# Idle products at the start, copies of gated banks, later squares of finished rows, and another order of the last block in a transformer-layer kernel

## The chip, the core and the metric

The kernel runs on one core of a Trainium2 chip. The time is the device time of one execution in microseconds; lower is better. Before the change it is 2542.43 us, the median of 3 runs (2542.26 to 2542.9).

Five engines work at once, each through its own queue in order: TensorE (PE, products), VectorE (DVE), ScalarE (ACT), GpSimd (POOL) and SyncE (SP), which issues most DMAs. A PE product adds `weights.T @ moving` into a bank of PSUM of 128 x 512 numbers; its weight load is shown as PEld.

## What is computed

One layer of a streaming encoder on x (2048 tokens of width 1024), all in float32:

```python
u = rms_norm(h, g_mix_pre)
z = u @ w_in                                  # 2816 columns: q, k, v, qh, fh, ih, gh
ya = swa_with_sinks(q, k, v, sinks)           # 8 heads, sliding window of chunks of 64
yh = hgrn2(qh, fh, ih, gh, lb, onorm)         # 4 heads, gated linear recurrence, chunkwise
y = concatenate([ya, yh]) @ w_out
h = h + rms_norm(y, g_mix_post)
u = rms_norm(h, g_x_pre); m = rms_norm(mem, g_mem)
y = cross_attention(u, m, wq, wk, wv, wo)     # 4 heads, 256 memory tokens
h = h + rms_norm(y, g_x_post)
u = rms_norm(h, g_ffn_pre)
y = (silu(u @ w_gate) * (u @ w_up)) @ w_down  # inner width 2816
h = h + rms_norm(y, g_ffn_post)
```

## The kernel before

**Products in three parts.** PE's fast format is fp32r. Each operand is split into `hi` (a copy rounded to fp32r) and `lo` (the rest), and a product is three: hi x hi, hi x lo, lo x hi. Those are lines 1167, 1168 and 1169 (`products`); the stationary side is a streamed tile S, the moving side a tile T. `split2` (L1027) makes the halves: `hi` on ACT (L1030) or POOL (L1032), `lo` always on DVE (L1033).

**Blocks.** The large matrix products run in blocks of two by two quarters. `seven` (L1171) computes such a block from seven products of combined quarters in place of eight; `STEPS` (L1023) gives the order of the seven for each kind of block. One step is one quarter product, 4 x 3 = 12 PE products where the inner width is 4 tiles. Products 1, 6, 7 and 4 gather in one PSUM bank, 5 and 3 in a second, 2 in a third. `copy` (L1178) takes the partial sums of 1, 6 and 5 out of their banks (L1182 on ACT; L1184 on DVE where a part of the result is added), and `out` gets the four results: (0,0) after product 2, (1,1) after 7, (0,1) after 3, (1,0) after 4. Kinds "o", "s" and "d" are such blocks; "d" runs two blocks at once, step by step. Kinds "p" and "q" use `eight` (L1211), plain products without sums. `streamed` (L1109) loads the S side and yields its halves in the order of the steps.

**The order of the work.** `phases` (L1248) runs all blocks of a list of jobs, step by step. After each step's products it makes the S tiles of two steps ahead (`upto(g + 2)`), advances what follows earlier blocks by one `yield` each (`after`), and splits and fetches the T tiles of later steps (`split`, `half`), so that one `yield` in an `after` is one step of PE. The rows that `after` handles and the fetched halves of T share nine buffers (`row_tile`, L1492). The whole program is one Tile program whose planner, from a model of times, sets the final order on each engine; `behind` (L1093) holds instructions behind others of their engine.

**The stages**, in order:

1. `in_first` (L445) projects the first 1024 tokens, 11 pairs of columns, from x itself, transposed on the host. The first three pairs are blocks of kind "p" whose rows aren't normed yet. `first(q, s)` splits one quarter of x into `hi` and `lo` in four chunks, each scaled by the gain (L468 on ACT, L469 on DVE). The loads are queued on SP by hand: the gain, the first weight block (`load` in `in_block`, L576), the four chunks of the first quarter of x (`between`), the second weight block, and so on.
2. `in_proj` projects the second 1024 tokens while attention and recurrence of the first run. `in_cols` (L708) multiplies 128 columns (L720, L721, L723) into a PSUM bank of kind "g", of which there are two. ACT takes its tanh (L728); for columns of qh and gh DVE then multiplies `(tanh + 1) * bank` (L733), reading the bank once more. Columns of fh get POOL's affine map, and their decays use tiles of tag "u".
3. Then come attention and recurrence of the rest, and the folding of the cross-attention's weights (`fold_cross`).
4. Three jobs of eight blocks of two token tiles (256 tokens): the out projection (`mixed_block`, L1541), the scores (`score_block`) and the values (`value_block`, L1623).
5. The feed-forward: hidden blocks for each half of the tokens, and three jobs of down blocks (`down_block`, L1726).

**After a block of 4** (L1554 and L1638). `squared` (L1528) writes a finished quarter into its row tile (L1532, L1534) and takes its squares on ACT (L1510). POOL turns the sums into a reciprocal root, DVE scales the rows (L1557, L1641), POOL issues a DMA that adds the residual from memory to the row (L1539), and SP stores it. Then, for n below 12, `rest` follows after one more `yield`: ACT's squares of the new row (L1510 by `mean_squares`), the root, in the value blocks a second scaled row (L1662), PE's transposes (L1421), ACT's copies out (L1422) and the store of the transposed row to `h1t_d` or `u_d`. For n of 12 and 14 `rest` runs beside the next job.

```python
            if n < NT - 4:
                yield
                yield from rest()
```

**The end.** The last down block (n = 14) writes the output. Each finished quarter (L1754, L1756) is squared on ACT (L1510) and multiplied by the gain (L1763); once both quarters of a row are there, POOL makes the root (L1766, L1769), DVE scales and adds the residual in two halves (L1772), and SP stores each.

Of the kernel before, what the change touches and what calls it, by code (L numbers as in the profile page):

```python
# [14 lines left out]
AF = mybir.ActivationFunctionType  # L15
ALU = mybir.AluOpType
AX = mybir.AxisListType

P = 128
T = 2048  # L20
# [8 lines left out]
NPB = TB // P  # L29
# [4 lines left out]
C_KA, C_VA, C_QH, C_FH, C_IH, C_GH = 512, 640, 768, 1280, 1792, 2304  # L34
# [14 lines left out]
class Layer:  # L49
# [229 lines left out]
    def consts(self):  # L279
        nc = self.nc  # L280
        self.ident = self.cst.tile([P, P], F32, name="ident")
        make_identity(nc, self.ident)
        self.mhalf = self.cst.tile([P, 8], F32, name="mhalf")
        nc.vector.memset(self.mhalf, -0.5)


# [158 lines left out]
    def in_first(self):  # L445
# [4 lines left out]
        u = [[], []]  # L450
        T, raw, second, stage = {}, {}, {}, []
        key = {(0, 0): 1, (1, 0): 2, (0, 1): 8, (1, 1): 3}
        self.r_bc = self.r_half = None
        self.held = True

        def tile():
            return self.pair_tile().rearrange("p a d -> p (a d)").rearrange("p (k t) -> p k t", k=4)

        def x_load(q, s):
            for k in range(4):  # L460
                self.load(raw[q, s][:, k, :], I["x_t"][2 * s + q, :, k, :])
# [74 lines left out]
        def parted():  # L536
            for n in (1, 3, 2, 0):
# [5 lines left out]
                with self.behind() if n else contextlib.nullcontext():  # L543
# [6 lines left out]
        blocks = [("p" if i < 3 else "o",)  # L550
                  + self.in_block(*p, beside[i], get if i > 6 else (), None if i else lambda: x_load(0, 0))
                  for i, p in enumerate(self.ORDER)]
# [22 lines left out]

    def in_block(self, ca, cb, beside, get, between):  # L576

# [130 lines left out]
    def in_cols(self, b, u, cols, e1):  # L708
        nc = self.nc
        w = []  # L710
        for c in cols:
            w.append(self.wcols(self.I["w_in"], c))
        z = [self.io_tile("z") for _ in cols]
        for s in range(TB // 512):
            sl = slice(s * 512, (s + 1) * 512)
            for i, c in enumerate(cols):
# [10 lines left out]
                else:  # L727
# [4 lines left out]
                    else:  # L732
                        nc.vector.scalar_tensor_tensor(zs, zs, 1.0, ps, ALU.add, ALU.mult)  # L733
                        if c0 < C_FH:
# [287 lines left out]

    STEPS = {"o": (1, 5, 6, 3, 7, 2, 4), "s": (1, 2, 5, 6, 7, 3, 4), "d": (1, 2, 5, 6, 7, 3, 4), "p": (1, 2, 8, 3), "q": (1, 2, 8, 3)}  # L1023
    TAKES = {"o": (1,) * 7, "s": (1,) * 7, "d": (1,) * 7, "p": (2, 2, 0, 0), "q": (4, 0, 0, 0)}
    BLOCK = {1: (0, 0), 8: (0, 1), 2: (1, 0), 3: (1, 1)}
# [83 lines left out]
    def streamed(self, load, nk, kind, engine=None, tiled=False):  # L1109
# [100 lines left out]

    def eight(self, S, T, nk, out, addend, halves=False):  # L1211
        a11, a21 = S[:2]
        x, y = self.bank("g"), self.bank("t")
# [214 lines left out]
    def jobs(self):  # L1428
# [112 lines left out]
    def mixed_block(self, n):  # L1541
# [12 lines left out]
        def after():  # L1554
# [6 lines left out]
            if n < NT - 4:  # L1561
                yield
                yield from rest()
# [59 lines left out]
    def value_block(self, n):  # L1623
# [14 lines left out]
        def after():  # L1638
# [6 lines left out]
            if n < NT - 4:  # L1645
                yield
                yield from rest()
# [186 lines left out]
```

## Time and profile before

| | us |
|---|---|
| median of 3 runs | 2542.43 |
| profiled execution | 2546.34 |
| its span, first to last instruction | 2544.6 |
| PE busy in the span | 2504.1 |
| DVE busy | 1765.3 |
| ACT busy | 1247.3 |
| POOL busy | 459.0 |

The mean granted TensorE clock of that execution is 0.998.

All lines come from one profiled execution, with times in us from the start of its span. A row of the timeline reads: start, duration, engine, line, operation, output <- inputs, shapes, and how many instructions were put together; in brackets the idle time of the engine before it and what ended it. SPq is SyncE issuing a DMA. "S L1030" as a releaser is the instruction of line 1030 that writes S.

### The profile page before, as it was taken

The page shows a single profiled execution, that of the slowest core. Times are in us where ns is not written, and L with a number is a line of the kernel's source. Part 1 is how long each engine was busy: PE and PEld are TensorE (multiplying, and loading weights), DVE is VectorE, ACT ScalarE, POOL GpSimd, SP SyncE. Part 2 cuts the span into 40 slices and gives each one's busy share as a digit, 9 for nine tenths or more (in the row PEclk, how much of TensorE's full clock was granted, in tenths as well). Part 3 has the DMA queues.
Part 4 walks back from the last instruction along what each step waited for, and adds up shares of the span by engine and source line. Part 5 has one row for each costly group of instructions (what it writes and reads, how often), then busy time and mean ns, then how long its engine had stood idle before and what let it go on. Part 6 is the DMA issues. An engine that isn't in the chain of part 4 may idle for free. (4 is left out here: it accounts for less than half of the span.)

```text
span 2544.6 us, 34410 instructions
## 1 busy us (share of the span) xinstructions
PE 2504.1 (98%) x12164; PEld 2096.0 (82%) x12164; DVE 1765.3 (69%) x2813; ACT 1247.3 (49%) x2598; POOL 459.0 (18%) x641
## 2 busy tenths in 40 slices
PE   8999999999999999999999999999999999999998
PEld 6777889988988878888788888888888888888786
DVE  6869587788777587787775665586566566665756
ACT  5454465566655566655554333353333344533443
POOL 2233233222422243233210000000000000000022
PEclk9999999999999999999999999999999999999999
DMA  6263544567896795859964532254555433667798
GB/s 240 96 216 139 174 141 137 170 201 223 292 326 211 208 288 176 299 174 265 302 206 143 180 132 92 91 177 151 177 207 187 153 132 135 209 199 203 218 223 209
DMA packets 267852, 490.00 MB, mean 193 GB/s; under 512 B 20640, under 2 KB 125088, under 8 KB 267168
## 3 DMA queue, kind: packets, MB, share of 16 engines
q1 hardware_dynamic: 253856, 438.52, 51.0%
q0 software_dynamic: 12672, 46.14, 9.0%
q10 hardware_dynamic: 1152, 3.15, 0.3%
q8 instruction: 96, 1.57, 0.3%
q14 instruction: 76, 0.62, 0.1%
HBM read 326.26 MB, written 161.48 MB: 192 GB/s over the span
## 5 line engine op out<-in xcount | busy, mean ns | idle before, releaser
L1167 PE MATMUL psm<-T,S 128*128 128x512 f32 x2744 | 1063.5, 392 | 9.8 <-ACT S L1030 3.8
L1168 PE MATMUL psm<-T,S 128*128 128x512 f32 x2744 | 1070.8, 390 | 0.0
L1169 PE MATMUL psm<-T,S 128*128 128x512 f32 x2744 | 1064.0, 391 | 4.4 <-DVE S L1033 4.1
L1167 PEld LDWEIGHTS psm<-T,S 128*128 128x128 f32 x2744 | 516.1, 188 | 121.7 <-ACT S L1030 5.2
L1169 PEld LDWEIGHTS psm<-T,S 128*128 128x128 f32 x2744 | 515.8, 188 | 116.3 <-DVE S L1033 9.0
L1168 PEld LDWEIGHTS psm<-T,S 128*128 128x128 f32 x2744 | 516.1, 188 | 106.3
L1030 ACT ACTIVATE S<-sum 128x512 fp32r<-128x512 f32 (+1 forms) x336 | 206.2, 618 | 328.8 <-PE psm L1169 326.7
L1033 DVE TENSOR_TENSOR S<-sraw,S 128x512 fp32r<-128x512 f32 (+1 forms) x312 | 211.1, 684 | 214.7 <-ACT S L1030 193.6
L1033 DVE TENSOR_TENSOR S<-sum,S 128x512 fp32r<-128x512 f32 (+1 forms) x400 | 272.0, 685 | 77.9 <-ACT S L1030 62.8
L1182 ACT ACTIVATE part<-psm 128x512 f32<-128x512 f32 x294 | 173.5, 593 | 184.2 <-PE psm L1169 181.0
L1030 ACT ACTIVATE S<-sraw 128x512 fp32r<-128x512 f32 (+1 forms) x271 | 165.6, 616 | 163.0 <-PE psm L1169 148.4
L1539 POOL DMA_DIRECT2D row<-y_d x28 | 25.0, 893 | 1072.4 <-DMA sraw<-hid_d 905.3
L1510 ACT ACTIVATE junk<-row 128x512 f32<-128x512 f32 x160 | 99.7, 625 | 95.7 <-DVE row L1532 33.2
L1033 DVE TENSOR_TENSOR T<-row,T 128x1024 fp32r<-128x1024 f32 x104 | 125.2, 1211 | 30.6 <-ACT T L1030 30.3
L1030 ACT ACTIVATE T<-row 128x1024 fp32r<-128x1024 f32 x104 | 105.5, 1024 | 27.2 <-DMA row<-in_w_down_dram 11.0
L720 PE MATMUL psg<-u,whi 128*128 128x512 f32 x288 | 115.8, 402 | 1.7 <-ACT z L726 1.3
L721 PE MATMUL psg<-u,whi 128*128 128x512 f32 x288 | 115.5, 401 | 0.0
L153 DVE TENSOR_TENSOR wlo<-raw,whi 128x1024 fp32r<-128x1024 f32 x54 | 70.5, 1310 | 32.1 <-ACT whi L150 14.8
L1714 DVE TENSOR_TENSOR part<-psm,part 128x512 f32<-128x512 f32 x66 | 45.5, 689 | 65.5 <-PE psm L1169 65.4
L1705 DVE TENSOR_TENSOR row<-psm,part 128x512 f32<-128x512 f32 x66 | 45.5, 689 | 53.8 <-PE psm L1169 53.8
L723 PE MATMUL psg<-u,wlo 128*128 128x512 f32 x288 | 79.9, 403 | 0.7 <-DVE wlo L153 0.7
L1032 POOL TENSOR_SCALAR S<-sum 128x512 fp32r<-128x512 f32 x64 | 49.2, 774 | 170.6 <-PE psm L1169 147.3
(347 smaller groups left out, 3562.2 us busy)
## 6 DMA issues: line engine op xcount, KB each, us to landing
sraw<-in_w_gate_dram SPq DMA_DIRECT2D x44, 512.0 KB, 4.8
sraw<-in_w_up_dram SPq DMA_DIRECT2D x44, 512.0 KB, 5.0
hid_d<-row SPq DMA_DIRECT2D x44, 512.0 KB, 2.7
h_d<-row SPq DMA_DIRECT2D x32, 512.0 KB, 7.1
y_d<-row SPq DMA_DIRECT2D x32, 512.0 KB, 3.8
sraw<-hid_d SPq DMA_DIRECT2D x32, 512.0 KB, 5.4
row<-h_d POOLq DMA_DIRECT2D x30, 512.0 KB, 7.9
row<-y_d POOLq DMA_DIRECT2D x28, 512.0 KB, 7.1
```

The source lines that it names most:

```text
L153: nc.vector.tensor_tensor(lo, raw, f32(hi), ALU.subtract)
L720: nc.tensor.matmul(ps, w[i][0][:, k, :], u[s][k][0], start=(k == 0), stop=False)
L721: nc.tensor.matmul(ps, w[i][0][:, k, :], u[s][k][1], start=False, stop=False)
L723: nc.tensor.matmul(ps, w[i][1][:, k, :], u[s][k][0], start=False, stop=(k == KT - 1))
L1030: self.nc.scalar.activation(hi, raw, AF.Copy)
L1032: self.nc.gpsimd.tensor_scalar(hi, raw, 1.0, 1.0, ALU.mult, ALU.mult)
L1033: self.nc.vector.tensor_tensor(lo, raw, f32(hi), ALU.subtract)
L1167: nc.tensor.matmul(ps, s[:, 0, k, :], t[:, 0, k, :], start=st, stop=False, **kw)
L1168: nc.tensor.matmul(ps, s[:, 0, k, :], t[:, 1, k, :], start=False, stop=False, **kw)
L1169: nc.tensor.matmul(ps, s[:, 1, k, :], t[:, 0, k, :], start=False, stop=sp, **kw)
L1182: nc.scalar.activation(t, ps, AF.Copy)
L1510: self.nc.scalar.activation(junk, a, AF.Square, scale=float(D) ** -0.5, accum_out=to)
```

## The change

There are six edits.

- **Early activation.** `consts` has ACT copy four numbers of `mhalf`, which DVE has set, to a small tile.
- **Idle products.** `in_first` starts with eleven PE products of `ident` with itself (128 x 128, float32), all into one PSUM bank that nothing reads.
- **Load order and `eight`.** Of the four chunks of x, the first is loaded behind the first weight block and the other three behind the second. In `eight`, the first two products of a "p" block run interleaved: for each of the four inner tiles, the three products of `a11` and the three of `a21`, in place of all twelve of `a11` and then all of `a21`.
- **Gated banks.** In `in_cols`, for qh and gh, ACT also copies the bank into a tile of tag "u", and DVE's multiply reads that copy.
- **Later squares.** For n = 8 and 10 of the out projection and the values, `rest` follows after three yields in place of one.
- **Last block.** The last down block has the kind "e": product 3 stands before product 7, and so do its S tiles (`streamed`); `TAKES` gets the same entry as the kinds beside it.

```diff
         nc.vector.memset(self.mhalf, -0.5)
+        nc.scalar.activation(self.small("w_mn", 4), self.mhalf[:, 0:4], AF.Copy)
...
         self.held = True
+        idle = self.bank("h")
+        for _ in range(11):
+            nc.tensor.matmul(idle[:, 0:P], self.ident, self.ident, start=True, stop=True)
...
-        def x_load(q, s):
-            for k in range(4):
+        def x_load(q, s, ks=range(4)):
+            for k in ks:
...
-                  + self.in_block(*p, beside[i], get if i > 6 else (), None if i else lambda: x_load(0, 0))
+                  + self.in_block(*p, beside[i], get if i > 6 else (), () if i else ((0,), (1, 2, 3)), x_load)
...
             for i, c in enumerate((ca, cb)):
-                if between and i and not j:
-                    between()
                 self.load(t[:, i, :], w[c, :, j * 512:(j + 1) * 512])
+                if between and not j:
+                    x_load(0, 0, between[i])
...
+        gated = not (cols[0] * P < C_QH or C_FH <= cols[0] * P < C_GH)
+        pre = self.io_tile("u") if gated else None
...
-                        nc.vector.scalar_tensor_tensor(zs, zs, 1.0, ps, ALU.add, ALU.mult)
+                        nc.scalar.activation(pre[:, sl], ps, AF.Copy)
+                        nc.vector.scalar_tensor_tensor(zs, zs, 1.0, pre[:, sl], ALU.add, ALU.mult)
...
+    STEPS = {..., "e": (1, 2, 5, 6, 3, 7, 4), ...}
...
-            yield made(combine(a11, a21, ALU.subtract), "P")
-            yield made(combine(a12, s2, ALU.subtract), "A")
+            last = [(a11, a21, "P"), (a12, s2, "A")]
+            for a, b, e in reversed(last) if kind == "e" else last:
+                yield made(combine(a, b, ALU.subtract), e)
...
-            self.products(x, [(a11, T[1], nk)], True, False)
-            self.products(y, [(a21, T[1], nk)], True, False)
+            kw = dict(skip_group_check=True)
+            for k in range(nk):
+                for ps, s in ((x, a11), (y, a21)):
+                    nc.tensor.matmul(ps, s[:, 0, k, :], T[1][:, 0, k, :], start=not k, stop=False, **kw)
+                    nc.tensor.matmul(ps, s[:, 0, k, :], T[1][:, 1, k, :], start=False, stop=False, **kw)
+                    nc.tensor.matmul(ps, s[:, 1, k, :], T[1][:, 0, k, :], start=False, stop=False, **kw)
...
-            last = "dd" if c + 1 < len(down) else ""
+            last = "dd" if c + 1 < len(down) else "e"
...
             if n < NT - 4:
-                yield
+                for _ in range(3 if n >= NPB else 1):
+                    yield
                 yield from rest()
```

The last hunk stands in `mixed_block` and in `value_block`. Before, the last block of the last job had kind "s": products 1, 2, 5, 6, 7, 3, 4.

More of the change, by code (lines that the diff above doesn't have):

```diff
@@ L574, in in_first, with in_block @@
         return u
-    def in_block(self, ca, cb, beside, get, between):
+    def in_block(self, ca, cb, beside, get, between, x_load):
         nc, w = self.nc, self.I["w_in"]
@@ L1016, in swa @@
             yield
-    STEPS = {"o": (1, 5, 6, 3, 7, 2, 4), "s": (1, 2, 5, 6, 7, 3, 4), "d": (1, 2, 5, 6, 7, 3, 4), "p": (1, 2, 8, 3), "q": (1, 2, 8, 3)}
-    TAKES = {"o": (1,) * 7, "s": (1,) * 7, "d": (1,) * 7, "p": (2, 2, 0, 0), "q": (4, 0, 0, 0)}
+    STEPS = {"o": (1, 5, 6, 3, 7, 2, 4), "s": (1, 2, 5, 6, 7, 3, 4), "d": (1, 2, 5, 6, 7, 3, 4), "e": (1, 2, 5, 6, 3, 7, 4), "p": (1, 2, 8, 3), "q": (1, 2, 8, 3)}
+    TAKES = {"o": (1,) * 7, "s": (1,) * 7, "d": (1,) * 7, "e": (1,) * 7, "p": (2, 2, 0, 0), "q": (4, 0, 0, 0)}
     BLOCK = {1: (0, 0), 8: (0, 1), 2: (1, 0), 3: (1, 1)}
@@ L1211, in eight @@
     def eight(self, S, T, nk, out, addend, halves=False):
+        nc = self.nc
         a11, a21 = S[:2]
@@ L1645, in after @@
             if n < NT - 4:
-                yield
+                for _ in range(3 if n >= NPB else 1):
+                    yield
                 yield from rest()
```

## The prediction

> **What bounds the kernel now.** The page comes first: one engine is busy nearly all the time, so of this change only what TensorE waits for can pay.
>
> ```profile
> span 2544.6 us, 34410 instructions
> PE 2504.1 (98%) x12164; PEld 2096.0 (82%) x12164; DVE 1765.3 (69%) x2813; ACT 1247.3 (49%) x2598; POOL 459.0 (18%) x641
> ```
>
> PE is idle for 2544.6 - 2504.1 = 40.5 us. The second view is the table of PE's waits: who was waited for, total us, times, longest us. These are its rows for places that the diff touches:
>
> ```profile
> PE psm L1167 <- ACT u L468: 8.2, 1, 8.2
> PE psm L1167 <- ACT S L1030: 3.8, 3, 2.6
> PE psm L1167 <- DVE row L1754: 2.2, 2, 1.3
> PE pss L1421 <- DVE row L1662: 1.5, 1, 1.5
> PE psg L720 <- DVE z L733: 0.4, 1, 0.4
> ```
>
> The first is the start, the second and fourth belong mostly to the value blocks, the third to the end, the fifth to the input projection's banks. The third view is the table of stretches: length, then busy us (and number) of PE, PEld, DVE, ACT and POOL, the granted clock, DMA share, GB/s.
>
> ```profile
> 8.16:11.58 3.42, 3.42 (x8) 2.40 (x8) 3.42 (x5) 2.56 (x5) 1.64 (x2) 1.00 1.03 373
> 1247.81:1254.01 6.20, 6.08 (x14) 4.34 (x14) 4.58 (x5) 5.03 (x10) 2.21 (x5) 0.50 1.02 359
> 1400.00:1500.00 100.00, 100.00 (x443) 82.80 (x442) 61.38 (x91) 35.35 (x62) 0.00 (x0) 1.00 0.55 180
> ```
>
> The last row is the normal pace, 100 / 443 = 0.226 us a product. The other two are slow: 3.42 / 8 = 0.43 us at the start, 6.20 / 14 = 0.44 us after the long wait in the middle, where the granted clock reads 0.50. (At the start it reads 1.00, but the pace says otherwise.) So a wait of 2.6 us costs more than itself.
>
> **The change part by part.** Sums go against the profiled execution, 2546.34 us (span 2544.6 and 1.74 around it), 3.91 above the median of 2542.43; what is saved there I take off the median.
>
> *Start* (early activation, idle products, load order, interleaved `eight`). The timeline from 0 to 16 us:
>
> ```profile
> 1.14 0.29 POOL masks.py:199 TENSOR_SCALAR_AFFINE_SELECT ident<-ident 128x128 f32<-128x128 f32 x1
> 6.00 1.28 ACT L468 ACT_TABLE_LOAD   x1 [6.00 <-DMA pair<-in_x_t_dram]
> 7.29 2.56 ACT L468 ACTIVATE u<-pair,g_t 128x512 fp32r<-128x512 f32 x4
> 8.16 0.77 PE L1167 MATMUL psm<-u,S 128*128 128x512 f32 x1 [8.16 <-ACT u L468]
> 9.76 0.61 ACT L1030 ACTIVATE S<-sraw 128x512 fp32r<-128x512 f32 x1
> 11.07 2.30 DVE L1033 TENSOR_TENSOR S<-sraw,S 128x512 fp32r<-128x512 f32 x3
> 15.32 0.39 PE L1169 MATMUL psm<-u,S 128*128 128x512 f32 x1
> ```
>
> The first x chunk is there at 6.00, but ACT loads its table until 7.28 before it touches it. The tiny activation on `mhalf` needs no DMA and pulls that load to about 1 us, under the wait for x. So the first product goes from 8.16 to 6.88, and the 24th, begun at 15.32, goes with it: 1.28. The Trainium skill (ScalarE: Activation LUTs, What ACT_TABLE_LOAD costs) counts a drain of about 1.38 us beside the load's 1.28, by which the saving would be 2.66; here ACT's first activation begins 1.29 after the load does, so the row decides.
>
> The idle products need `ident`, so they start at about 1.5. Two rows of PE's timeline price them:
>
> ```profile
> 1229.36 1.06 PE L1421 MATMUL pss<-ident,row 128*128 128x128 f32 x8 [1.47 <-DVE row L1662]
> 1247.81 0.79 PE L1167 MATMUL psm<-T,S 128*128 128x512 f32 x1 [2.59 <-ACT S L1030]
> ```
>
> Eight transposes of that shape take 1.06 us, so eleven take at most 1.5 at full clock, 2.9 at half: they end by 4.4. But the pace rose only after 3.42 us of products, and it was down after 2.59 us of idleness. At most 2.9 us of idle products, with about 2.5 of idleness behind them, should not have the clock up at 6.88; I count them at nothing. If they do raise it, the operands set the rate: with the second weight block third in line, DVE's five splits, at 2.30 / 3 us each from 6.7 on, feed products until 10.4, and the 24th begins near 12.6, a saving of 2.7. The other end: the interleaving makes the fourth product need `a21`, where it was the thirteenth. If ACT still splits that behind four chunks (9.76 less 1.28), DVE's half is ready near 10.5, and 18 more products at 0.23 put the 24th at 14.7, a saving of 0.6. **1.3**, ends 0 (rivals) and 2.7. In the other two blocks of `eight` the same products run in another order: nothing.
>
> *Value blocks 8 and 10.* From the timelines of DVE, POOL, ACT and SP:
>
> ```profile
> 1234.67 2.47 DVE L1641 SCALAR_TENSOR_TENSOR row<-row,q_r,g 128x1024 f32<-128x1024 f32 x2
> 1236.30 0.93 POOL L1539 DMA_DIRECT2D row<-h_d  x1 [5.92 <-DVE row L1641]
> 1220.58 0.63 ACT L1510 ACTIVATE junk<-row 128x512 f32<-128x512 f32 x1 [4.94 <-DMA row<-h_d]
> 1244.47 0.63 ACT L1510 ACTIVATE junk<-row 128x512 f32<-128x512 f32 x1 [2.77 <-DMA row<-h_d]
> 1239.07 7.30 SPq L75 DMA_DIRECT2D row<-u_d  x2
> ```
>
> Block 10's rows are normed at 1234.67, the adding DMA is issued at 1236.30, and its row is there at 1244.47, 9.8 us on. The squares stand three steps behind the norm, 3 x 12 x 0.226 = 8.1 us, so ACT stands still for 2.77. Queued behind it is the split of an S that PE waits for until 1247.81: 2.59 us. Block 8 does the same (4.94 at 1220.58); there the chain goes over rstd and DVE's norm to PE's transposes, 1.47 us. Two steps more (5.4 us) make 13.6 us, beyond the 9.8, and nothing here needs the rows sooner: the tokens of these blocks are read by the second half of the feed-forward alone. What goes: 1.47 + 2.59, and the slow products of 1247.81 to 1254.01, 6.20 - 14 x 0.226 = 3.0. Together 7.1.
>
> What is late next: the rows. The squared rows stay in their buffers 5.4 us longer, and their transposed stores are issued 5.4 later. SP already stands for most of 7.30 us at a load into a row buffer, with ACT's split of that row some steps on. I set 0.8 against this: **6.3**, ends 0 and 7.1, below nothing in a rival.
>
> *Out projection's blocks 8 and 10.* One short stall has the same cause:
>
> ```profile
> 901.61 0.63 ACT L1510 ACTIVATE junk<-row 128x512 f32<-128x512 f32 x1 [0.70 <-DMA row<-in_x_dram]
> 907.60 0.50 PE L1167 MATMUL psm<-T,S 128*128 128x512 f32 x1 [0.37 <-ACT S L1030]
> ```
>
> Four squares and 0.70 us of standing precede the split that PE waits for. **0.4**, ends 0 and 1.
>
> *Gated banks.* Sixteen copies of 0.59 us are added; DVE's multiply frees 16 banks now and would no longer:
>
> ```profile
> L728 ACT ACTIVATE z<-psg 128x512 f32<-128x512 f32 x24 | 14.2, 590 | 5.8 <-PE psg L723 5.7
> L733 DVE SCALAR_TENSOR_TENSOR z<-z,psg 128x512 f32<-128x512 f32 x16 | 10.9, 678 | 0.0
> ```
>
> PE waited for that multiply once, 0.4 us. The copies are 16 x 0.59 = 9.4 us of ACT, which beside these banks stood for PE itself (5.7 us before the 24 activations). The far ends are -9.4 (each copy delays PE) and 0.4; ACT's cover being in the rows, I take **0** and keep -2, five copies without cover less what is gained.
>
> *End* (kind "e"). The timelines of DVE, ACT and PE:
>
> ```profile
> 2529.63 0.68 DVE L1754 TENSOR_TENSOR row<-psm,part 128x512 f32<-128x512 f32 x1
> 2531.83 0.69 DVE L1754 TENSOR_TENSOR row<-psm,part 128x512 f32<-128x512 f32 x1 [1.51 <-PE psm L1169]
> 2532.60 0.63 ACT L1510 ACTIVATE junk<-row 128x512 f32<-128x512 f32 x1 [6.71 <-issue]
> 2532.66 0.47 PE L1167 MATMUL psm<-T,S 128*128 128x512 f32 x1 [0.88 <-DVE row L1754]
> 2535.26 0.39 PE L1169 MATMUL psm<-T,S 128*128 128x512 f32 x1
> 2535.54 1.41 DVE L1772 SCALAR_TENSOR_TENSOR row<-row,p_r,row 128x512 f32<-128x512 f32 x2 [0.87 <-POOL p_r L1769]
> 2536.87 0.68 DVE L1756 TENSOR_TENSOR row<-psm,row 128x512 f32<-128x512 f32 x1
> ```
>
> PE's last step waits for the output at 2531.83, so that was product 7, and product 3 (output 2529.63) already ran ahead of it. Only ACT keeps the written order: it holds the square of row 0's finished half until 2532.60. Row 0 is then finished at 2535.54 to 2536.95 on DVE, just when the last product, ended at 2535.65, needs DVE. With the square at 2530.3, POOL and DVE finish row 0 some 2 us sooner, under the last product, and 2536.87 becomes 2535.7: **1.1**, ends 0 and 1.2. PE's 0.88 stays.
>
> Sum: 1.3 + 6.3 + 0.4 + 0 + 1.1 = 9.1, so 2542.43 - 9.1 = **2533.3 us**.
>
> **The rivals.**
>
> *The clock stays down as long as in the middle.* The slow stretch lasted 3.42 us at the start, but some 6.2 from 1247.81 on. If it lasts 6.2 from 6.88, the 15th product starts near 13.1 and the 24th at 15.2: the start gives 0.1, the time is 2542.43 - 0.1 - 6.3 - 0.4 - 1.1 = 2534.5. For and against it: one of the two slow rows each; the start's own is nearer. Chance 0.15. The Trainium skill (TensorE: Matmul & The Clock Gate, The HAM clock gate) says that activity is judged in free-running windows of about 3.4 us, so that the slow stretch varies from run to run; the two stretches here, 3.42 and 6.20 us, agree with that.
>
> *The idle products raise the clock:* the start gives 2.7, the time is 2531.9. For it: the idleness before 6.88, about 2.5 us, is a little under the 2.59 that cooled it. Against it: 2.9 us of products are fewer than 3.42. Chance 0.10.
>
> *A row's split takes the squares' place.* ACT's queue near 1247 also holds splits of rows that SP loads; if one of them stands for its DMA, half of the value blocks' gain is left, 3.2: 2542.43 - 1.3 - 3.2 - 0.4 - 1.1 = 2536.4. For it: SP's 7.30 us. Against it: no row's split stands among ACT's waits quoted from 1220 to 1248. Chance 0.13.
>
> *One new wait.* If the buffer that SP waits for comes free 5.4 us later, a row lands 5.4 later, ACT stands as long at its split, and PE idles about as long (2.77 of ACT made 2.59 of PE), with 3.0 of slow products behind: 8.4 against 7.1 saved, 1.3 lost. Time: 2542.43 - 1.3 - 0.4 - 1.1 + 1.3 = 2540.9. Chance 0.12.
>
> *Slower.* The same mechanism for both value blocks: 16.8 us against 7.1, so +9.7 less 2.8, or 2549.3. It decides once ACT's slack before a row's split is under the 5.4 us of the longer hold; SP's 7.30 us speak for it; against it, that nine buffers turn over there and that ACT stood only at squares in the rows above. Chance 0.08.
>
> *It doesn't do what it says:* the order on an engine is the planner's, and added copies may move instructions anywhere before 760 us; that is the -2 above.
>
> **How the numbers follow.** The forecast itself has 0.42; the clock rivals 0.15 and 0.10, the split 0.13, one new wait 0.12, two 0.08. A measurement of this kernel tells 0.2% (5.1 us) from no change, so faster means under 2537.3 and slower over 2547.5. Faster: 0.42 + 0.15 + 0.10 and two thirds of 0.13, less a little for the parts' low ends: 0.75. Slower: the two new waits and 0.01 for the copies, 0.09. Same: the rest, 0.16. Range: down to 2528.5, every best end (2.7 + 7.1 + 1 + 0.4 + 1.2 = 12.4, 2530.0) and 1.5 for other waits that the new plan happens to drop; up to 2541, which takes in one new wait and leaves two out.
>
> **What would show it.** ACT's table load at about 1 us and the first product near 6.9; the pace of the first eight products; no DMA before ACT's squares (L1510) after 1200, no wait over 1 us near 1247, clock 1.00 there; the last L1756 within 0.1 us of the last product. Wrong would be: a new wait for ACT's split of T, or longer standing of SP at a row load, between 1200 and 1300.

## The result, and the profile after

The change makes the kernel slower: 2560.19 us, the median of six runs (2550.17 to 2563.73), against 2542.66 beside it; ratio 1.0064 with a 95% interval of 1.0054 to 1.0074. Forecast were 2533.3 us and at most 2541. The profiled execution took 2563.73 us. In the changed kernel lines stand up to 15 lower down: L1037, L1040, L1177, L1190 and L1523 are L1030, L1033, L1169, L1182 and L1510 of before.

First the page, then the table of PE's waits, of the changed kernel:

```profile
span 2561.8 us, 34459 instructions
PE 2514.9 (98%) x12186; PEld 2104.4 (82%) x12186; DVE 1761.5 (69%) x2813; ACT 1255.0 (49%) x2615; POOL 460.1 (18%) x641
```

```profile
PE psm L1175 <- ACT part L1190: 8.8, 6, 4.4
PE psm L1175 <- ACT S L1037: 6.8, 3, 5.8
PE psg L726 <- ACT z L732: 3.3, 1, 3.3
```

PE is idle for 46.9 us (40.5 before), and its busy time is 10.8 longer, of which 4.9 are the idle products and most of the rest slow clock behind waits. The 8.2 us at the start and the 1.5 for the rows are gone from the table; ACT has taken their place.

To see where, I compare stretches between the same PE products (counted from the first one, idle products left out), in us. The columns begin at 0, 246, 562, 863 and 1202 us of before:

| kernel | start to 189 | 246-292 | 562-713 | 863-995 | 1202-1308 | behind the last product's start |
|---|---|---|---|---|---|---|
| before | 188.9 | 45.7 | 151.3 | 132.1 | 106.6 | 9.38 |
| after | 186.8 | 50.4 | 156.9 | 135.3 | 115.2 | 8.20 |
| difference | -2.1 | +4.6 | +5.6 | +3.2 | +8.6 | -1.2 |

Of the rest, the stretch from 1308 to 2379 us takes 1070.77 in every trace of this study, and the one behind it 153.9 in place of 156.3, which is the longest of all traces: that execution of before stood there for itself. The first and the last column came as forecast or better. The value blocks, forecast at -6.3, give +8.6. Two stages in which I forecast nothing lose 10.2 together.

*The start.* The timelines of ACT and PE:

```profile
0.79 1.28 ACT L285 ACT_TABLE_LOAD   x1 [0.79 <-PEq L1841]
5.78 0.72 ACT L472 ACTIVATE u<-pair,g_t 128x512 fp32r<-128x512 f32 x1 [3.49 <-DMA pair<-in_x_t_dram]
1.49 4.91 PE L458 MATMUL pss<-ident 128*128 128x128 f32 x22 [1.49 <-POOL ident masks.py:199]
6.65 0.95 PE L1240 MATMUL psm<-u,S 128*128 128x512 f32 x2 [0.24 <-ACT u L472]
13.15 0.40 PE L1242 MATMUL psm<-u,S 128*128 128x512 f32 x1
```

Eleven idle products are 22 records of 0.223 us, so they reach 6.40, not 4.4, and leave 0.24 us of idleness. From 7.44 on products start 0.23 to 0.25 us apart where operands allow. The last row is the 24th product: 2.17 us sooner than before, against a forecast of 1.3 and a rival's 2.7. The twelve traces without the early activation have that product at 15.32 to 17.55 us, and 15.32 is the kernel before's own, so 2.17 is the low end of what the start gained.

*246 to 292 us.* ACT's timeline of the changed kernel, then of a kernel in which the planner's order is that of before (experiment h1_idle6):

```profile
258.56 0.63 ACT L802 ACTIVATE qs<-qd 128x512 fp32r<-128x512 f32 x1 [11.25 <-DMA qd<-z_d]
259.09 0.58 ACT L732 ACTIVATE z<-psg 128x512 f32<-128x512 f32 x1
```

```profile
251.88 0.60 ACT L730 ACTIVATE z<-psg 128x512 f32<-128x512 f32 x1 [3.52 <-PE psg L727]
259.35 0.63 ACT L799 ACTIVATE qs<-qd 128x512 fp32r<-128x512 f32 x1 [6.87 <-DMA qd<-z_d]
```

The bank's tanh now stands behind a copy of queries, which stands 11.25 us for a load. PE gets its bank back late and waits 3.3 us, and then runs slowly: 8 products in 3.3 us.

```profile
259.70:263.00 3.30, 3.28 (x8) 2.60 (x9) 1.49 (x2) 0.00 (x0) 1.25 (x1) 0.50 0.33 94
```

No gated bank is near, and the edits do not touch these instructions: their place in the planned order has changed.

*The value blocks.* ACT's waits from 1200 to 1330 us, then the timelines of SP, ACT and PE:

```profile
ACT T L1037 <- DMA row<-u_s: 11.6, 4, 10.0
ACT junk L1523 <- DMA row<-h_d: 8.1, 5, 4.7
ACT T L1037 <- DMA row<-u_d: 6.5, 1, 6.5
```

```profile
1249.49 0.36 SPq L78 DMA_DIRECT2D u_d<-row  x1
1256.48 3.87 SPq L78 DMA_DIRECT2D h_d<-row  x2
1261.27 0.37 SPq L75 DMA_DIRECT2D row<-u_d  x1
1267.32 1.06 ACT L1037 ACTIVATE T<-row 128x1024 fp32r<-128x1024 f32 x1 [6.51 <-DMA row<-u_d]
1269.62 0.76 PE L1175 MATMUL psm<-T,S 128*128 128x512 f32 x1 [4.37 <-ACT part L1190]
1284.06 0.36 SPq L78 DMA_DIRECT2D u_d<-row  x1
1295.20 0.81 SPq L75 DMA_DIRECT2D row<-u_s  x2
1302.96 1.06 ACT L1037 ACTIVATE T<-row 128x1024 fp32r<-128x1024 f32 x1 [10.02 <-DMA row<-u_s]
1309.93 0.80 PE L1175 MATMUL psm<-T,S 128*128 128x512 f32 x1 [5.78 <-ACT S L1037]
```

A transposed store of block 8 is issued at 1249.49 and has landed at 1261.20; only then does SP issue the load into that buffer. The row arrives at 1267.3, ACT has stood for it 6.5 us, and PE behind ACT 4.4. Block 10 repeats it at 1284.06. This is the "slower" rival's mechanism, at both its places. At the second, the load is issued at 1295.20, right after the store's landing at 1295.14, with no store of first rows (h_d) ahead of it. Of the 8.1 us at squares in the table 5.0 are block 6's, which the change does not move; blocks 8 and 10 stand 3.1 us, against 8.4 before.

### The profile page after: what moved, and what is told of

Same layout as the page of the kernel before. It is cut to its first block, busy times and chain, and to the rows that moved or that the text cites. A ratio compares the mean times of both kernels' runs of the same rounds, so it can differ in the third digit from the quotient of the medians.

```text
span 2561.8 us, 34459 instructions
## 1 busy us (share of the span) xinstructions
PE 2514.9 (98%) x12186; PEld 2104.4 (82%) x12186; DVE 1761.5 (69%) x2813; ACT 1255.0 (49%) x2615; POOL 460.1 (18%) x641
## 5 line engine op out<-in xcount | busy, mean ns | idle before, releaser
L1177 PE MATMUL psm<-T,S 128*128 128x512 f32 x2744 | 1065.2, 391 | 5.0 <-DVE S L1040 4.9
L1177 PEld LDWEIGHTS psm<-T,S 128*128 128x128 f32 x2744 | 516.3, 188 | 116.3 <-DVE S L1040 8.5
L1037 ACT ACTIVATE S<-sum 128x512 fp32r<-128x512 f32 (+1 forms) x336 | 206.0, 618 | 325.3 <-PE psm L1177 323.2
L1040 DVE TENSOR_TENSOR S<-sraw,S 128x512 fp32r<-128x512 f32 (+1 forms) x312 | 211.5, 685 | 213.1 <-ACT S L1037 192.4
L1040 DVE TENSOR_TENSOR S<-sum,S 128x512 fp32r<-128x512 f32 (+1 forms) x400 | 271.5, 684 | 77.3 <-ACT S L1037 63.3
L1190 ACT ACTIVATE part<-psm 128x512 f32<-128x512 f32 x294 | 173.5, 593 | 185.8 <-PE psm L1177 181.7
L1037 ACT ACTIVATE S<-sraw 128x512 fp32r<-128x512 f32 (+1 forms) x271 | 165.6, 616 | 175.0 <-PE psm L1177 165.0
L1040 DVE TENSOR_TENSOR T<-row,T 128x1024 fp32r<-128x1024 f32 x104 | 124.5, 1204 | 38.9 <-ACT T L1037 38.6
L1523 ACT ACTIVATE junk<-row 128x512 f32<-128x512 f32 x160 | 99.7, 625 | 69.8 <-DVE row L1545 18.2
L1037 ACT ACTIVATE T<-row 128x1024 fp32r<-128x1024 f32 x104 | 105.4, 1023 | 41.1 <-DMA row<-in_w_down_dram 12.6
L1720 DVE TENSOR_TENSOR row<-psm,part 128x512 f32<-128x512 f32 x66 | 45.5, 689 | 55.8 <-PE psm L1177 55.7
```

What stands on the lines that cost most here:

```text
L1037: self.nc.scalar.activation(hi, raw, AF.Copy)
L1040: self.nc.vector.tensor_tensor(lo, raw, f32(hi), ALU.subtract)
L1177: nc.tensor.matmul(ps, s[:, 1, k, :], t[:, 0, k, :], start=False, stop=sp, **kw)
L1190: nc.scalar.activation(t, ps, AF.Copy)
L1523: self.nc.scalar.activation(junk, a, AF.Square, scale=float(D) ** -0.5, accum_out=to)
```

## The experiments

Theories. **A:** a row buffer held two steps longer delays SP's load of a T row, and ACT stands there. **B:** SP's in-order queue delays the load, behind stores that wait for adding DMAs. **C:** what is lost comes from the planner's order, not from any instruction's cost. Ratios are to the kernel before, run in the same series.

### The parts by themselves

**Later squares alone** (e1_squares), in both stages:

```diff
-                yield
+                for _ in range(3 if n >= NPB else 1):
+                    yield
```

> The kernel before with the later squares alone, in both stages; the other five edits are left out. Theory A (a row's buffer is held two steps longer, SP's load of the next T row waits for it, ACT stands at that row's split, PE behind ACT): nothing differs ahead of 860 us; the out projection's blocks lose some 3 us and the value blocks 8 to 9 us, as the profile of the changed kernel has it, so about 2554.5 us, ratio 1.0047; PE waits for ACT near 1265 and 1305, with ACT standing at T splits (L1037 there, L1030 here) for DMAs of rows. Rival B (the value blocks' loss comes from where the stages ahead of them had been shifted, and the squares themselves gain the forecast 6.7): about 2536 us.

2551.29 against 2540.79, ratio 1.0042 (1.0029 to 1.0054). The planner's order differs on no engine ahead of 860 us, so the loss is the squares' own. A's size was a little high.

**Copies alone** (e2_gated):

```diff
-                        nc.vector.scalar_tensor_tensor(zs, zs, 1.0, ps, ALU.add, ALU.mult)
+                        nc.scalar.activation(pre[:, sl], ps, AF.Copy)
+                        nc.vector.scalar_tensor_tensor(zs, zs, 1.0, pre[:, sl], ALU.add, ALU.mult)
```

> The kernel before with the gated banks' copies on ACT alone. Theory A: the planner's order first differs near the first copy (480 us or later), and the stretch from 560 to 720 us loses the 5 to 6 us that the changed kernel lost there; nothing near 259 us and nothing behind 900; about 2548 us, ratio 1.002. Rival B (the copies are hidden beside PE's own work and the loss from 560 to 720 us belongs to the shifted start): 2542.5 us, ratio 1.000.

2544.85 against 2540.79, ratio 1.0012 (1.0003 to 1.0021): a loss of about 3 to 4 us, between the two theories' 2548 and 2542.5. One row of the groups has all 16 copies:

```profile
L735 ACT ACTIVATE u<-psg 128x512 f32<-128x512 f32 x16 | 9.5, 594 | 0.0
```

Their duration was forecast (9.4 us). The stretch from 562 to 713 us takes 153.1 to 156.9 in the three traces with copies, and 149.4 to 154.5, mean 151.5, in the twelve without them that keep nine row buffers: the two ranges overlap, so the place of the loss is likely, not shown. The first copy stands at 372 us, sooner than I had put it, and ACT's order begins to differ there; from some 525 us on (DVE) and 570 us on (ACT) the order differs in dozens of places. Whether the order or the copies themselves cost, and where, is not settled.

**The start alone** (e3_start): early activation, idle products, load order and interleaving, as in the diff.

```diff
+        nc.scalar.activation(self.small("w_mn", 4), self.mhalf[:, 0:4], AF.Copy)
...
+        for _ in range(11):
+            nc.tensor.matmul(idle[:, 0:P], self.ident, self.ident, start=True, stop=True)
...
+                if between and not j:
+                    x_load(0, 0, between[i])
```

> The kernel before with the three edits of the start: early activation, idle products, load order with the interleaved products. Theory A: the first 220 us gain 2, and the planner, given another start, moves ACT's copy of the queries (qs) ahead of a bank's copy near 259 us and PE loses 4.6 there; together about 2545 us, ratio 1.001. Rival B (the swap near 259 us belongs to the gated copies): 2540.5 us, ratio 0.999.

2542.22 against 2540.79, ratio 1.0005 (0.9996 to 1.0014). Its trace reaches the product at 189 us at 186.6, and then spends 47.7 us on the stretch from 246, where all traces without the swap have 45.5 to 46.1. The swap is here, without any copies: rival B of this run falls. Theory A had the swap right and its price too high: 2.0 us here, where the changed kernel lost 4.6. PE waits as long in both, 3.34 and 3.32 us; the difference is the clock behind the wait (rows at the end).

**Early activation and last block alone** (e4_act_last):

```diff
+        nc.scalar.activation(self.small("w_mn", 4), self.mhalf[:, 0:4], AF.Copy)
...
-            last = "dd" if c + 1 < len(down) else ""
+            last = "dd" if c + 1 < len(down) else "e"
```

> The kernel before with the early activation and the last block's new order alone. Both theories: 1.3 us at the start and 1.1 at the end, with the order of all engines between as before, so 2540 us, ratio 0.9990. If the planner's order mattered even where it does not differ, or the first 1.3 us were lost again at the waits near 250 and 267 us, 2541.5.

2539.03, ratio 0.9993 (0.9984 to 1.0002). As forecast in size, though the interval still holds no change.

**Six idle products** (h1_idle6), with the early activation and the last block. Load order and interleaving are left out.

```diff
-        for _ in range(11):
+        for _ in range(6):
```

> The early activation, six idle products in place of eleven, and the last block's new order, on the kernel before; load order, interleaving, copies and later squares are left out. With six idle products the planner's order of SP and ACT stays that of before. Theory: the products end near 4.1 us, 2.8 ahead of the first real product; if the clock holds over that, the first 24 products come out 1.5 us sooner than with the early activation alone, so 2537 to 2538 us, ratio 0.998. Rival: the clock is down again, 2539 to 2540 us as the early activation and last block alone.

2540.00 against 2541.84, ratio 0.9991 (0.9983 to 1.0000). Some 2 us faster than before, at the edge of what was measured, and not to be told from e4_act_last's 0.9993. Its 246-292 stretch is back at 45.7, without the swap; whether the load order, the interleaving or the other five idle products bring it, no run shows. PE's timeline of its start:

```profile
1.49 2.93 PE L458 MATMUL pss<-ident 128*128 128x128 f32 x12 [1.49 <-POOL ident masks.py:199]
7.08 0.76 PE L1172 MATMUL psm<-u,S 128*128 128x512 f32 x1 [2.66 <-ACT u L472]
```

After 2.93 us of idle products and 2.66 of idleness the eight products from 7.08 to 10.50 take 0.43 us each: the clock rival of this run was right. Eleven products (4.91 us, 0.24 of idleness) had them at 0.23. That agrees with the Trainium skill (TensorE: Matmul & The Clock Gate, The HAM clock gate), by which the full clock takes a busy window of about 3.4 us.

**The later squares undone from the changed kernel** (i1_undo_squares):

```diff
-                for _ in range(3 if n >= NPB else 1):
-                    yield
+                yield
```

> The changed kernel with its later squares undone in both stages; start, copies and last block stay. On every engine its order is that of the start edits and of the copies put together, with nothing of its own. If the parts add: 10 to 11 us less than the changed kernel, some 4 over the kernel before, about 2546 us, ratio 1.0015 to 1.002. Rival (the squares cost more on a shifted start, as the profile of the changed kernel has 8.9 us in the value blocks and the squares alone about 4): 2543 us or less.

2544.39 against 2541.91, ratio 1.0012 (1.0003 to 1.0021). With e1's 1.0042 that makes 1.0054 against the change's 1.0064 (1.0054 to 1.0074): the parts add within what was measured. Between the medians the squares cost 15.8 us on the changed kernel (2560.19 against 2544.39) and 10.5 alone; that they cost more beside the other edits is possible and not shown.

### Which squares

**Value blocks alone** (e6_val) and **out projection alone** (e7_mix): the hunk of e1 in `value_block` or in `mixed_block` only.

```diff
 def value_block / mixed_block:
+                for _ in range(3 if n >= NPB else 1):
+                    yield
```

> The kernel before with the later squares in the value blocks alone. The squares in both stages gave 2551.3 against 2540.8. Theory A (a row buffer held two steps longer delays SP's load of a T row): the value blocks carry most of it, 7 to 8 us, so about 2548 us, ratio 1.003; ACT stands over 4 us at a T split for a row's DMA between 1240 and 1310 us. Rival (the out projection's blocks carry it, and the value blocks gain what was forecast): about 2535 us.

> The kernel before with the later squares in the out projection's blocks alone. Theory A: the same hold of buffers costs 2 to 3 us at the scores' first T rows near 955 us, so about 2543.3 us, ratio 1.001, with nothing changed from 1200 us on. Rival: it gains the forecast 0.4, 2540.4 us, or it carries most of the 10.5 us, 2550 us.

Values: 2549.00 against 2542.47, ratio 1.0025 (1.0014 to 1.0036). Out projection: 2547.11, ratio 1.0015 (1.0007 to 1.0024). Both lose; the out projection's share was forecast at half. ACT's waits from 1200 to 1330 us, in e6_val and, with the squares where they were, in h1_idle6:

```profile
ACT T L1030 <- DMA row<-u_s: 6.0, 3, 4.9
ACT T L1030 <- DMA row<-u_d: 4.8, 1, 4.8
ACT junk L1510 <- DMA row<-h_d: 3.8, 3, 2.6
```

```profile
ACT junk L1515 <- DMA row<-h_d: 9.2, 4, 5.7
ACT T L1034 <- DMA row<-u_s: 1.7, 2, 1.2
```

So the wait for squares did fall, from 9.2 to 3.8 us; 10.8 us of waiting for T rows replaced it. But it fell at block 8, from 6.7 us to 0.6. Block 10's squares still stand for the adding DMA: 2.6 us in e6_val, 2.5 in h1_idle6, 2.8 before (and 2.1 in e1_squares and in the changed kernel). ACT in e6_val:

```profile
1248.61 0.63 ACT L1510 ACTIVATE junk<-row 128x512 f32<-128x512 f32 x1 [2.64 <-DMA row<-h_d]
```

They begin 10.3 us after block 10's norm (1238.27), not the forecast 13.6: later in ACT's order is not as much later in time. Three splits of T rows stand ahead of them where one stood, and ACT runs these without a wait. PE still waits 1.66 us behind the squares, at 1250.51, where it waited 2.59.

**A or B?** Two tries to take one of them away, both with the value blocks' later squares. In f2_val_inplace blocks 8 and 10 scale their rows in place, two row buffers fewer each; in g1_val_h2late the stores to h_d are written two steps later:

```diff
-            u = [self.row_tile() for _ in range(2)]
+            u = [y[i] if NPB <= n < NT - 4 else self.row_tile() for i in range(2)]
```

```diff
+                for i in range(2 if n >= NPB else 0):
+                    self.store(self.h2_d[(n + i) * P:(n + i + 1) * P, :], y[i])
```

> Later squares in the value blocks alone, and blocks 8 and 10 write their second scaled rows over the first ones (u is y itself), so that each block takes two row buffers fewer; DVE's scaling then also waits for the store of the first rows. Theory A (the buffers): SP's T rows no longer wait for the transposed store, ACT stands under 2 us at any T split near 1240 to 1310 us, the stalls for the squares are gone as well, and 4 of the forecast 7.1 us (the profiled execution was 5.5 above the median, so some of its stall was its own) come out: about 2537 us, ratio 0.9985. Rival B (SP's queue: the rows' stores h_d stand in it for the adding DMA, and the loads behind them): as the later squares in the value blocks alone, 2547 to 2548 us.

> Later squares in the value blocks alone, and the stores of the first rows (to h2_d) of blocks 8 and 10 are issued two steps later too, when the adding DMA has long landed, so that SP need not stand for it; the buffers are held as long as before or longer. Rival B (SP's queue): the loss is gone, about 2537 us, ratio 0.9985. Theory A (the buffers): within 2 us of the later squares in the value blocks alone, 2546 to 2549 us.

2546.69, ratio 1.0018 (1.0009 to 1.0026), and 2546.11, ratio 1.0013 (1.0004 to 1.0022). The second is no test: the planner put those stores where they had been, and the order on every engine is e6_val's; it is a second sample of it. Together they put the value blocks' loss at 1.3 to 2.5 thousandths, 3.6 to 6.5 us. f2_val_inplace came out close to rival B's time, which alone would speak for the queue; SP's timelines show why taking the buffers away changed little. In e6_val and in f2_val_inplace:

```profile
1240.02 0.36 SPq L78 DMA_DIRECT2D u_d<-row  x1
1248.54 3.05 SPq L78 DMA_DIRECT2D h_d<-row  x2
1251.70 0.37 SPq L75 DMA_DIRECT2D row<-u_d  x1
```

```profile
1243.78 0.33 SPq L78 DMA_DIRECT2D h_d<-row  x1
1244.21 0.42 SPq L78 DMA_DIRECT2D u_d<-row  x1
1246.43 0.33 SPq L78 DMA_DIRECT2D h_d<-row  x1
1246.81 0.77 SPq L75 DMA_DIRECT2D row<-u_d  x1
```

In e6_val the transposed store lands at 1251.26, and the second h_d store is issued at 1251.26, its adding DMA having landed; the T load behind both goes at 1251.70. The two holds end together. In place, the load needs no buffer from that store any more, and still stands behind the h_d store until 1246.43. At block 10's own place in e6_val only the buffer holds: the transposed store issued at 1274.11 lands at 1280.66, and the load follows at 1280.72.

**Both away** (h3_val_row10): ten row buffers, paid for with one raw S buffer; and the same without the later squares as a control (h4_row10).

```diff
-        return self.st_pool.tile([P, D], F32, tag="row", name=f"row_{self._n}", bufs=9)
+        return self.st_pool.tile([P, D], F32, tag="row", name=f"row_{self._n}", bufs=10)
...
-                self.raws, self.parts, self.sums = 6, 4, 5
+                self.raws, self.parts, self.sums = 5, 4, 5
```

> Later squares in the value blocks alone, with ten row buffers for nine, paid for by five raw S buffers for six. In the order of SP that comes out, the four loads of T rows from u_d and one from u_s stand ahead of both stores of block 10's first rows (h_d) and of the transposed stores; with nine buffers only three do, and the fourth stands behind a transposed store's landing and both h_d stores, which wait for the adding DMA. Theory A+B (the load is held twice at the same time, by its buffer and by SP's queue, so that taking one away shows nothing): both are gone, ACT stands under 2 us at T rows from 1240 to 1265 us, and the kernel is 3 to 5 us faster than the same kernel without the later squares (the control with ten buffers), and 5 to 8 us faster than the later squares with nine. Rival C (the loss comes from the squares' new place on ACT itself): as with nine buffers, 4 to 6 us over the control.

> Control: the kernel before with ten row buffers and five raw S buffers, no other change. The planner's order differs from 860 us on. If nine buffers bind nothing before the change: within 2 us of the kernel before, 2541 to 2544. If five raw S buffers cost something, up to 2550; if rows wait for buffers already before the change (SP's 7.30 us at the row load), 2538.

2544.90, ratio 1.0012 (1.0003 to 1.0021), and the control 2543.37, ratio 1.0012 (1.0004 to 1.0021). With the tenth buffer the later squares cost nothing that can be measured in the run times: 1.5 us between the medians, and the 4 to 6 us of that run's rival C (the squares' new place on ACT) are not seen. SP and ACT in h3_val_row10:

```profile
1238.39 7.16 SPq L75 DMA_DIRECT2D row<-u_d  x4
1253.55 0.33 SPq L78 DMA_DIRECT2D h_d<-row  x1
```

```profile
ACT T L1030 <- DMA row<-u_s: 1.2, 1, 1.2
```

All four loads from u_d stand ahead of the h_d stores, and ACT waits 1.2 us for T rows in place of 10.8. So A and B together account for the waits for T rows. The gain of 3 to 5 us that I expected over the control did not come, and the stretch from 1202 to 1308 us is still 106.8 in this trace against 103.7 in the control's. PE waits for splits of S instead, 1.73 us for DVE at 1255.58, 1.0 for ACT at 1291 and 1.2 for DVE at 1293. Ten buffers are not free either: the planner's order differs from 734 us on, and the stretch from 863 to 995 us takes 135.0 and 135.1 in these two, longer than in any trace with nine buffers and the out projection's squares where they were. That is why h3_val_row10 is read against its control and not against the kernel before.

**One step later in place of two** (e8_val2):

```diff
+                for _ in range(2 if n >= NPB else 1):
```

> Later squares in the value blocks, one step in place of two (2.7 us). In SP's order the fourth T load stands behind a transposed store but ahead of both h_d stores. Theory A+B: half of the hold, so the loads are some 3 us late in place of 6, the stalls for the squares are gone, and the sum lies within 2 us of the kernel before: 2541 to 2544 us, ratio 1.000. Rival C (any move of the squares costs its 5 us, by the order on ACT): 2547 us.

2542.58 against 2541.84, ratio 1.0001 (0.9993 to 1.0010): no loss, no gain, as theory A+B had it. There the fourth T load stands ahead of both h_d stores. The loss begins between 2.7 and 5.4 us of delay.

### The out projection

**A second look** (i2_mix_again, e7_mix's kernel) and **one step in place of two** (i3_mix_one, e8's edit in `mixed_block`).

```diff
 def mixed_block:
+                for _ in range(2 if n >= NPB else 1):
```

> The later squares in the out projection alone, once more, for the profile of a second execution. Theory: an execution near the median (2545 to 2548 us) shows 3 to 5 us more than the kernels without this edit between 860 and 1000 us, at T or S tiles of the scores that are late on DVE. Rival: that stretch is as long as in the others, and the loss, if there is one, lies elsewhere or comes and goes.

> Later squares in the out projection alone, one step in place of two. If what costs is the length of the hold, as in the value blocks: no loss, 2541 to 2543 us, ratio 1.000. If any other order there costs the same: 2546 to 2547 us, ratio 1.0015.

2545.41 against 2541.91, ratio 1.0017 (1.0007 to 1.0027); one step 2547.79, ratio 1.0020 (1.0011 to 1.0029). So here the length of the hold is not what costs. The stretch from 863 to 995 us takes 135.2 in the second look; in ten traces with nine buffers and the squares where they were it takes 129.7 to 132.4. Of the other traces with the edit, i3_mix_one has 133.3 and the changed kernel 135.3, but e1_squares 131.7 and e7_mix 130.4 lie inside that range (e7_mix's profile is the fastest of its eleven runs). So the loss is measured in the run times, and its place is seen in three of five traces. The DMA views of i2_mix_again from 893 to 915 us and of e4_act_last from 889 to 910 us (count, size, median us from issue to landing) show what differs:

```profile
row<-in_x_dram POOLq DMA_DIRECT2D x2, 512.0 KB, 10.7
```

```profile
row<-in_x_dram POOLq DMA_DIRECT2D x2, 512.0 KB, 7.1
```

The adding DMA itself lands later. For block 10's first row it takes 6.4 to 8.0 us in the traces without this edit, 8.5 to 9.8 in the four with it, and 11.1 with one step. In SP's new order loads of T rows (qk_d) go out just ahead of it or beside it: one in e4_act_last (6.4 us), two in i2_mix_again (9.8), three in i3_mix_one (11.1). The squares were moved two steps away from the DMA, and the DMA moved after them; POOL, ACT and PE in i2_mix_again:

```profile
896.98 0.94 POOL L1539 DMA_DIRECT2D row<-in_x_dram  x1
906.89 0.63 ACT L1510 ACTIVATE junk<-row 128x512 f32<-128x512 f32 x1 [3.91 <-DMA row<-in_x_dram]
909.74 0.50 PE L1167 MATMUL psm<-T,S 128*128 128x512 f32 x1 [1.53 <-ACT S L1030]
953.48 0.60 ACT L1606 ACTIVATE row<-row,x_mr,r_x 128x256 f32<-128x256 f32 x1 [2.50 <-POOL x_mr L1604]
954.66 0.57 ACT L1182 ACTIVATE part<-psm 128x512 f32<-128x512 f32 x1
```

The squares still stand 3.91 us, with the same split of S behind them as before, and PE loses 1.53 where it lost 0.37. The last two rows belong to a second loss, 2.42 us of PE at 955.38: a part's copy behind an exponential whose maximum comes late from DVE. The changed kernel has the same 2.42 at 961.55. That the loads lengthen the adding DMA is read from these traces and was not isolated. It would agree with the Trainium skill (DMA: Bandwidth & Descriptors, Issuing engines are not separate DMA queues): whoever issues them, DMAs run on the same engines and interleave.

## Why the prediction was wrong

- **Value blocks, forecast 6.3 saved: the wrong step.** It was "I set 0.8 against this", with 0 as the worst end. The experiments give 3.6 to 6.5 us lost for these blocks alone, and nothing measurable with a tenth buffer. I had the row that says so (SP standing 7.30 us at a row load) and the mechanism, as the rival "Slower", with its condition: ACT's slack before a row's split under the 5.4 us of the longer hold. Its argument against, that no row's split waited, held only for the stretch quoted, 1220 to 1248. The condition could have been read off the trace of before. The load that SP issued at 1246.02, just after a transposed store's landing (1245.96), arrived at 1251.11, and ACT split that row at 1251.31 (the first line): 0.2 us of slack, and 2.7 at the same place in h1_idle6. At the next row, at 1256.39, ACT stood 3.5 us (the second line, of ACT's waits from 1210 to 1260 us):

```profile
1251.31 1.05 ACT L1030 ACTIVATE T<-row 128x1024 fp32r<-128x1024 f32 x1
ACT T L1030 <- DMA row<-u_s: 3.5, 1, 3.5
```

  While ACT stood at squares, the rows arrived: what a wait ahead of it creates is not slack.
- **Value blocks, "what goes: 1.47 + 2.59", and 3.0 of slow products:** a second step that failed. The squares' place was reckoned in steps of PE (13.6 us against the DMA's 9.8); block 10's came 10.3 us behind the norm in e6_val and 9.7 in the changed kernel and still stood, and 5.6 of the 7.1 us hung on that block.
- **The saving itself was too large besides.** The profiled execution was 3.91 us over its median. Its stretch from 1202 to 1308 us took 106.6; eight other traces with these squares where they were (and nine buffers) took 103.9 to 105.6, mean 104.9, and the five with the squares two steps later (and nine buffers) 107.3 to 115.2. Some 1.6 of the 7.1 us belonged to that one execution.
- **Out projection, 0.4 saved:** lost 3.5 to 4.6 instead. The duration of the adding DMA was held fixed; under the new order of SP's loads it was some 2 us longer, and the squares stood 3.91 us (i2_mix_again) in place of 0.70.
- **Gated banks, 0 with -2 as the end:** about -3 to -4. The 9.4 us of copies were sized well. What failed is the step from "beside these banks ACT stood for PE" to 0: it looked at the copies and not at what the planner would make of them. That its order is what costs is argued, not shown.
- **Start, 1.3 saved:** about 2 at the 24th product and at 189 us, and then a term that the sum did not have, the swap at 259 us, which took 2.0 (e3_start) to 4.6 (after). The pricing of idle products by transposes (0.13 us each) was wrong by a factor of 3.4: a float32 product of `ident` is two records of 0.223 us. The rival in which they raise the clock was right on the clock; then the operands set the pace, as it had it, and the 24th product came at 13.15 in place of its 12.6, ACT having stood 0.55 and 1.05 us for later chunks of x.
- **End, 1.1 saved: right.** From the start of the last product to the end of the span 9.38 us became 8.20, and 8.18 to 9.05 in the three other traces with the new order, against 9.37 to 9.39 in all without it. DVE now scales row 0 from 2551.08 on, beside PE's last twelve products:

```profile
2551.08 1.42 DVE L1787 SCALAR_TENSOR_TENSOR row<-row,p_r,row 128x512 f32<-128x512 f32 x2 [0.21 <-POOL p_r L1784]
```

- **The chances.** "It doesn't do what it says" named the planner and priced it at -2. The start's edits moved its order at a price of 2.0 to 4.6 us by the traces, and the copies came with 3 to 4 us lost, against gains of some 3 at the two ends of the kernel. The copies' place, "before 760 us", was right; that the start's edits would move the order was in no term.

What stays open: what in the copies or their order costs; which of the start's edits brings the swap; why the squares' saving does not come once the rows' waits are gone; and the second loss near 955 us, which was seen in two traces and not isolated.

## What to carry to other kernels

When a wait on an in-order engine is to be removed, list what else arrives during it: whatever sits behind it has been hidden by it, and a longer hold of a shared buffer is a later load. Measure the slack as the time from a row's landing to its use, not by the absence of a wait. Where two holds end at the same moment, taking one away shows nothing; take away both, or the source, before calling the theory wrong. Under a planner, compare the planned order of every engine first: an edit of 1 us at the start can swap two instructions 250 us later and lose what it gains, or more.

## What the hardware showed beyond that

- A pause's length does not set its price. Two waits of PE of 2.42 us at the same place left the clock at 1.00 (i2_mix_again, 16 products in 3.62 us) and at 0.54 (the changed kernel, 9 in 3.45). Two of 3.3 us at the swap left it at 1.00 (e3_start, 15 in 3.40) and at 0.50 (the changed kernel, the row of 259.70 above):

```profile
955.38:959.00 3.62, 3.62 (x16) 3.02 (x17) 3.10 (x5) 1.47 (x3) 0.00 (x0) 1.00 0.44 149
961.55:965.00 3.45, 3.45 (x9) 2.76 (x10) 2.49 (x4) 0.86 (x2) 0.00 (x0) 0.54 0.58 157
259.60:263.00 3.40, 3.40 (x15) 2.75 (x16) 1.55 (x2) 0.00 (x0) 1.31 (x1) 1.00 0.32 94
```

  Shorter waits can cost it too: in h1_idle6, after 1.96 us at 1245.15 and 0.60 at 1246.49, products from 1247.04 to 1249.60 start 0.43 us apart.

- A transposed store of 512 KB took 11.2 us from issue to landing in the full DMA traffic of the value blocks (e6_val, the 16 engines 95.7% busy from 1239 to 1242 us), longer than the two adding DMAs beside it (8.6 and 10.1), so a buffer's release lies far behind its last use.

- Executions of the changed kernel lie 13.6 us apart, those of e4_act_last 5.7: one profiled execution prices a stall only to a few us. That each DMA that PE can see adds its own scatter is argued, not shown.
